# A hybrid decoder step on one core: both scans' stages of a turn in one row on TensorE, and pairs of PSUM banks begun together in the preparation

## The chip, the cores and the metric

The kernel runs on 1 core of one Trainium2 chip. The metric is the device time of one launch in microseconds (us). PE is TensorE, PEld its weight loads, DVE VectorE, ACT ScalarE, POOL GpSimd, SP SyncE; ACTq is ACT's sequencer when it issues a DMA.

## The reference

One layer of a decoder is computed for 1024 prompt tokens and 64 sample tokens (8 sequences of 8), all in fp32. The part that the change touches is the mixer: two recurrent scans that share one projection of the input and one projection of the output.

```python
proj = x @ w_in
o_a, ... = _rwkv7_mix(proj[..., :A_SHIFT_W], ...)          # mixer A: 8 heads of 64
o_b, ... = _gated_delta_mix(proj[..., A_SHIFT_W:], ...)    # mixer B: 4 heads of 128
mix = jnp.concatenate([o_a, o_b], axis=-1) @ w_o
x = _layer_norm(DN_ALPHA * x + mix, ln1_g, ln1_b)
ffn, f_conv_new = _conv_ffn(x, f_conv, w_up, f_conv_w, f_conv_b, w_down)
x = _layer_norm(DN_ALPHA * x + ffn, ln2_g, ln2_b)
e = _rms_norm(p @ w_ple, ple_g)
x = x + jax.nn.sigmoid(x @ w_ple_gate) * e
```

Mixer A updates a matrix state `S = S * w_t + sa (kk_t * a_t) + v_t k_t` token by token; mixer B works in chunks, `v_new = u_c - w_c @ S`, `o = q_c @ S + a_c @ v_new`, `S = S * gl + k_c^T v_new`, after a triangular solve in each chunk.

## The kernel before, in words

**Two kinds of work on PE.** The dense products (projections, output projection, feed-forward, gate) are fp32r products of 128x512: each weight and each activation is split into a high and a low part, and three products are added up. They are recorded on PE as `acc<-x,whi`, `acc<-x,wlo`, `acc<-whi,X` and so on, one record each. Everything of the two scans and their preparation is plain fp32, and each such product leaves two records on PE, a transpose one.

**Units.** The prompt is cut into two blocks of 512 tokens (`tb`), each into two halves of 256 (`half`), and the heads into two groups (`g`). `run` (L1609) goes through eight prompt units: for each block first both halves of group 0, then both of group 1, and then two small sample units. I number the prompt units 1 to 8; units 1 to 4 belong to the first block.

- `prep` (L1047) prepares a unit: shifts, gates and norms, then `a_gram` (L673: Gram products `aux<-AR,BK`, transposes `aux<-cst,BK` and `aux<-cst,tmp`), `b_gram` (L822: Gram products `aux<-BK,KN`, DVE's product into `MB`, transposes `aux<-cst,KN` and `aux<-cst,tmp`), and `invert` (L947). `invert` sends the triangular systems through DRAM (DMAs `inv_t`, then `iN`), solves 16x16 blocks on DVE in some 30 small steps from `iY<-iN` to `iN<-iY`, and loads the result back (DMAs `inv_x`, `inv_y`, then 8 loads `Dt<-inv_y` and 8 `Dd<-inv_x`), all DMAs issued by ACT.
- `merge` (L996) builds the inverses of the larger blocks from that: four rounds of PE products with an addition on DVE behind each (`aux<-Dt,MG`, `aux<-Dd,DX`, `aux<-Y,DX` twice), then three smaller steps. A row of a round begins with `touch` (L204, `aux<-zeros`), a product that waits for all that the row needs.
- `scan` (L1069) runs mixer A's four chunks and mixer B's two, with the merge of the next unit beside them.
- `out` (L899) normalises the outputs and writes them to DRAM; its first product on PE is `aux<-OA,cst`.

**The scans' stages.** `a_step` (L735) has three stages with a yield behind each: R (`scan<-S,AR`, `scan<-UV,MG`), solve (`scan<-RA,DX`), and out with the state (`scan<-AR,S`, `scan<-MG,UV` into one bank, `scan<-UV,BT` into another). `b_step` (L874) has R (`scan<-S,KN`), solve (`scan<-RB,DX`) and out with the state (`scan<-QE,S`, `scan<-MB,UB` into one bank, `scan<-UB,KD` into another), each followed by two yields. `together` (L717) advances all generators by one yield in each turn. So in turn 1 A's R meets B's R, in turn 3 A's out meets B's solve, in turn 5 A's solve meets B's out, and so twice per unit.

**PSUM.** There are eight banks: four of the pool `acc` for the dense products, two of `aux` for the preparation, the merge and `out`, two of `scan` for the scans. ACT or DVE must empty a bank before it is used again.

**What sets the order.** The kernel is written as a program whose instructions a list scheduler orders, engine by engine, by priority and by when operands are ready in its own model; each engine then runs its list strictly in order. Inside `fill` (L263) instructions get a low priority, so that dense products fill PE between the scans' steps. In the first block the fill is the rest of the projection of the second block and the embedding product; the output projection `dense_first` (L1410) can begin with the two features of 128 rows that group 0 wrote, and its further features, and all that comes behind it, need what the `out` of unit 4 writes. A row (`inrow`, L198) chains the matmuls issued in it, so that they keep the order in which they are written:

```python
def mm(s, out, lhsT, rhs, start=True, stop=True):
    i = s.nc.tensor.matmul(out, lhsT=lhsT, rhs=rhs, start=start, stop=stop)
    if s.row is not None:
        if s.row:
            s.tc.add_manual_dep(i.ins, s.row[-1], s.nosync, reason="order")
        s.row.append(i.ins.name)
```

A chain only says what comes first on PE. It does not forbid other instructions in between.

Of the kernel before, what the change touches and what calls it, by code (L numbers as in the profile page):

```python
# [145 lines left out]
class Kern:  # L146
# [40 lines left out]
        return s.bank("scan")  # L187

    def mm(s, out, lhsT, rhs, start=True, stop=True):
        i = s.nc.tensor.matmul(out, lhsT=lhsT, rhs=rhs, start=start, stop=stop)  # L190
        if s.row is not None:
            if s.row:
                s.tc.add_manual_dep(i.ins, s.row[-1], s.nosync, reason="order")
            s.row.append(i.ins.name)
        return i
# [15 lines left out]

    def tr(s, out, in_):
        k = in_.shape[0]
        s.nc.tensor.transpose(out, in_, s.ident[:k, :k])  # L214

    def act(s, out, in_, f=AF.Copy, **kw):
        s.nc.scalar.activation(out, in_, f, **kw)  # L217
# [455 lines left out]
    def a_gram(s, st, cm):  # L673
        nc = s.nc
        nch, AR, BK, Xv = st["nch"], st["AR"], st["BK"], st["Xv"]
        last = nc.cur_bb.bb.instructions[-1]
        MG = s.tl([128, NCH, 2, 2, 2, 64], "MG", 2)
        st["room"] = MG.rearrange("p c a s e t -> p (c a s e t)")[:, 512:1664].rearrange("p (i x) -> p i x", i=2)
        MG = MG[:, :nch]
        BT = s.tl([128, NCH, 2, 128], "BT", 2)[:, :nch]  # L680
        UV = s.tl([128, NCH, 2, 2, 64], "UV", 2)[:, :nch]
        for e in range(2):
            nc.gpsimd.memset(UV[64 * (1 - e):64 * (1 - e) + 64, :, :, e, :], 0.0)
        cc = min(nch, 2)
        n = 2 * cc
        mask = s.cst[:, cm:cm + 128].rearrange("p (s t) -> p s t", s=2).unsqueeze(1).broadcast_to([128, n, 2, 64])
        for c0 in range(0, nch, 2):
            bs = [s.bank() for _ in range(2)]
            with s.inrow():
                s.touch(bs[1], last)  # L690
                for i in range(n):
                    c, p = c0 + i // 2, i % 2
                    for e, b in enumerate(bs):
                        r = 64 * e
                        s.mm(b[:, i * 128:(i + 1) * 128], BK[r:r + 64, p, c, :, :], AR[r:r + 64, p, c, 1:3, :])
            for e, b in enumerate(bs):
                s.mul(MG.rearrange("p c a s e t -> p (c a) s e t")[:, 2 * c0:2 * c0 + n, :, e, :],
                      b[:, :n * 128].rearrange("p (h s t) -> p h s t", h=n, s=2), mask)
        for c0 in range(0, nch, 2):
            b = s.bank()  # L700
            for i in range(n):
                c, p = c0 + i // 2, i % 2
                s.tr(b[:, i * 128:(i + 1) * 128], BK[:, p, c, :, :].rearrange("p s t -> p (s t)"))
            s.act(BT[:, c0:c0 + cc].rearrange("p c a t -> p (c a t)"), b[:, :n * 128])

        b = s.bank()
        nq = nch // cc
        for i in range(2 * nq):
            q, p = i // 2, i % 2
            s.tr(b[:64 * cc, i * 128:(i + 1) * 128], Xv[:, p, q * 64 * cc:(q + 1) * 64 * cc])  # L710
        b = b[:, :nq * 256].rearrange("p (q a e v) -> p q a e v", q=nq, a=2, e=2)
        for e in range(2):
            for i in range(cc):
                s.act(UV[64 * e:64 * e + 64, i::cc, :, e, :], b[64 * i:64 * i + 64, :, :, e, :])
        st.update(MG=MG, BT=BT, UV=UV)

    def together(s, *gens):  # L717

        gens = list(gens)
        while gens:  # L720
            gens = [g for g in gens if next(g, True) is None]

    def a_solve(s, st, c, R):

# [97 lines left out]
    def b_gram(s, st, cn):  # L822
        nc = s.nc
        KN, KQ, Xv, tm, gd, t0, m, nq, g = (st[k] for k in ("KN", "KQ", "Xv", "tm", "gd", "t0", "L", "nq", "g"))
        q0 = t0 // 128
        n = 2 * nq
        hs = slice(2 * g, 2 * g + 2)
        M = s.tl([128, 2, 2, 2, LB], "MB", 2)[:, :nq, :, :, :m]
        KD = s.tl([128, 2, 256], "KD", 2)[:, :nq]
        VB = s.tl([128, 2, 256], "VB", 2)[:, :nq]  # L830
        E = s.tmp(128, nq, 2, m)
        for q in range(nq):
            nc.sync.dma_start(E[:m, q], gd[2:3, hs, t0 + q * m:t0 + (q + 1) * m].broadcast_to([m, 2, m]))
        for q in range(nq):
            for h in range(2):
                s.stt(E[:m, q, h, :], E[:m, q, h, :], tm[:m, q0 + q, 0, 2 * g + h:2 * g + h + 1], s.cst[:m, cn:cn + m],
                      ALU.subtract, ALU.add)
        Ef = E[:m].rearrange("p q h t -> p (q h) t")
        s.act(Ef, Ef, AF.Exp)
        for q in range(nq):  # L840
            b = s.bank()
            for h in range(2):
                s.mm(b[:m, h * 2 * m:(h + 1) * 2 * m], KN[:, h, q * m:(q + 1) * m], KQ[:, h, q, :, :])
            s.mul(M[:m, q], b[:m, :4 * m].rearrange("p (h s t) -> p h s t", h=2, s=2),
                  E[:m, q].unsqueeze(2).broadcast_to([m, 2, 2, m]))
        for src, dst, kind in ((KN, KD, 3), (Xv, VB, 1)):
            b = s.bank()
            for q in range(nq):
                for h in range(2):
                    j = 2 * q + h  # L850
                    s.tr(b[:m, j * 128:(j + 1) * 128], src[:, h, q * m:(q + 1) * m])
            s.mul(dst[:m].rearrange("p q (h d) -> p q h d", h=2), b[:m, :n * 128].rearrange("p (q h d) -> p q h d", q=nq, h=2),
                  tm[:m, q0:q0 + nq, kind, hs].unsqueeze(3).broadcast_to([m, nq, 2, 128]))
        st.update(MB=M, KD=KD, VB=VB)
# [214 lines left out]
    def scan(s, tb, half, g, st, ahead):  # L1069

        sa, sb, Z = st
        OA = s.tl([128, 2, MB], "OA")
        OB = s.tl([128, 2, MB], "OB")

        def a_all():
            for c in range(NCH):
                yield from s.a_step(sa, c, OA)
                yield

        def b_all():  # L1080
            for q in range(MB // LB):
                yield from s.b_step(sb, q, OB)

        s.together(a_all(), b_all(), *ahead)
        return OA, OB

    def mix_out(s, tb, half, g, st, o):
# [646 lines left out]
```

## Time and profile before

| | |
|---|---|
| median of 3 runs | 1921.58 us (1918.12 to 1926.15) |
| the profiled execution's own time | 1920.4 us |
| its span | 1918.6 us, 29879 instructions |
| PE busy | 1831.8 us (95%), 10446 records |
| DVE, ACT, POOL busy | 1269.8, 918.0, 154.7 us |
| granted clock of PE, mean | 0.989 |
| DMA | 255.88 MB, mean 133 GB/s |

A row of the timeline has the start of the first record, the time to the end of the last, engine, line, operation, what it writes and reads, shapes and the number of records; in brackets stands the engine's idle time before it and what ended that. Records of PE overlap: a product of 128x512 lasts about 0.4 us as a record, while the next begins 0.23 us later.

### The profile page before, as it was taken

The page shows a single profiled execution, that of the slowest core. Times are in us where ns is not written, and L with a number is a line of the kernel's source. Part 1 is how long each engine was busy: PE and PEld are TensorE (multiplying, and loading weights), DVE is VectorE, ACT ScalarE, POOL GpSimd, SP SyncE. Part 2 cuts the span into 40 slices and gives each one's busy share as a digit, 9 for nine tenths or more (in the row PEclk, how much of TensorE's full clock was granted, in tenths as well). Part 3 has the DMA queues.
Part 4 walks back from the last instruction along what each step waited for, and adds up shares of the span by engine and source line. Part 5 has one row for each costly group of instructions (what it writes and reads, how often), then busy time and mean ns, then how long its engine had stood idle before and what let it go on. Part 6 is the DMA issues. An engine that isn't in the chain of part 4 may idle for free. (4 is left out here: it accounts for less than half of the span.)

```text
span 1918.6 us, 29879 instructions
## 1 busy us (share of the span) xinstructions
PE 1831.8 (95%) x10446; PEld 1463.3 (76%) x10446; DVE 1269.8 (66%) x2748; ACT 918.0 (48%) x1814; POOL 154.7 (8%) x305
## 2 busy tenths in 40 slices
PE   9999999999799798999999999999999999999998
PEld 7878777777567577777887767777787888888877
DVE  4366566758586685877768767666857752455488
ACT  5454447465564744646455435543633332333372
POOL 2000010001000000000000000200212210111000
PEclk9999999999899899999999999999999999999999
DMA  6435342434444365442423446875332222222355
GB/s 216 152 123 153 112 113 89 137 100 133 144 138 145 126 181 163 129 114 82 117 81 112 131 137 194 274 246 200 134 119 92 96 78 83 83 78 79 114 174 165
DMA packets 219126, 255.88 MB, mean 133 GB/s; under 512 B 81848, under 2 KB 117096, under 8 KB 218976
## 3 DMA queue, kind: packets, MB, share of 16 engines
q1 hardware_dynamic: 162040, 246.36, 39.8%
q10 hardware_dynamic: 56936, 7.62, 2.5%
q8 instruction: 82, 1.34, 0.3%
q14 instruction: 68, 0.56, 0.1%
HBM read 200.64 MB, written 53.26 MB: 132 GB/s over the span
## 5 line engine op out<-in xcount | busy, mean ns | idle before, releaser
L190 PE MATMUL acc<-x,whi 128*128 128x512 f32 x2400 | 784.5, 403 | 7.9 <-ACT whi L217 5.1
L220 DVE TENSOR_TENSOR wlo<-wraw,whi 128x512 fp32r<-128x512 f32 (+1 forms) x462 | 323.2, 700 | 343.7 <-ACT whi L217 319.0
L217 ACT ACTIVATE whi<-wraw 128x512 fp32r<-128x512 f32 (+1 forms) x462 | 287.4, 623 | 497.8 <-PE acc L190 169.0
L190 PEld LDWEIGHTS acc<-x,whi 128*128 128x128 f32 x2400 | 429.5, 189 | 89.0 <-issue 7.8
L190 PE MATMUL acc<-x,wlo 128*128 128x512 f32 x1200 | 483.0, 403 | 0.0
L190 PEld LDWEIGHTS acc<-x,wlo 128*128 128x128 f32 x1200 | 226.9, 189 | 54.3 <-issue 6.0
L190 PE MATMUL acc<-whi,X 128*128 128x512 f32 x436 | 145.5, 407 | 9.5 <-ACT st L217 6.2
L217 ACT ACTIVATE st<-acc 128x512 f32<-128x512 f32 (+2 forms) x134 | 77.4, 595 | 62.3 <-PE acc L190 39.2
L190 PEld LDWEIGHTS acc<-whi,X 128*128 128x128 f32 x436 | 81.9, 191 | 29.8 <-ACT st L217 7.2
L190 PE MATMUL acc<-wlo,X 128*128 128x512 f32 x220 | 87.5, 398 | 0.0
L229 DVE SCALAR_TENSOR_TENSOR st<-st,par,st 128x512 f32<-128x512 f32 (+1 forms) x132 | 78.1, 593 | 2.8
L217 ACT ACTIVATE st<-st 128x512 f32<-128x512 f32 x66 | 33.3, 505 | 72.9 <-DVE st L229 68.4
L190 PE MATMUL scan<-whi,X 128*128 128x256 f32 (+2 forms) x208 | 62.4, 335 | 0.0
L217 ACT ACTIVATE tmp<-tmp 128x512 f32<-128x512 f32 (+4 forms) x75 | 40.5, 548 | 30.6 <-DVE tmp L229 22.7
L229 DVE SCALAR_TENSOR_TENSOR st<-st,st 128x512 f32<-128x512 f32 x74 | 40.6, 550 | 19.5 <-ACT st L217 18.6
L190 PE MATMUL scan<-whi,xsm 128*128 128x256 f32 x176 | 49.3, 281 | 2.4 <-ACT st L217 2.4
L190 PE MATMUL scan<-wlo,X 128*128 128x256 f32 (+2 forms) x164 | 51.5, 314 | 0.0
L217 ACT ACTIVATE X<-wraw 128x512 fp32r<-128x512 f32 (+1 forms) x65 | 40.5, 623 | 21.1 <-DMA wraw<-hd 10.7
L506 POOL COPY tail<-st 128x3 f32<-128x3 f32 x52 | 14.6, 283 | 436.6 <-ACT st L217 436.6
L220 DVE TENSOR_TENSOR X<-wraw,X 128x512 fp32r<-128x512 f32 x60 | 43.5, 724 | 9.4 <-ACT X L217 9.3
L217 ACT ACTIVATE tmp<-tmp,par 128x256 f32<-128x256 f32 (+1 forms) x100 | 43.0, 470 | 14.0 <-issue 4.5
L190 PE MATMUL scan<-wlo,xsm 128*128 128x256 f32 x176 | 49.5, 282 | 0.0
(358 smaller groups left out, 3306.9 us busy)
## 6 DMA issues: line engine op xcount, KB each, us to landing
wraw<-w_up SPq DMA_DIRECT2D x176, 256.0 KB
wraw<-w_in SPq DMA_DIRECT2D x112, 256.0 KB
wraw<-w_down SPq DMA_DIRECT2D x98, 256.0 KB
wraw<-hd SPq DMA_DIRECT2D x44, 256.0 KB
wraw<-w_o SPq DMA_DIRECT2D x32, 256.0 KB
wraw<-w_gate SPq DMA_DIRECT2D x32, 256.0 KB
hd<-st SPq DMA_DIRECT2D x22, 256.0 KB
st<-lnv SPq DMA_DIRECT2D x20, 256.0 KB
```

Source lines behind the costliest of these rows:

```text
L190: i = s.nc.tensor.matmul(out, lhsT=lhsT, rhs=rhs, start=start, stop=stop)
L217: s.nc.scalar.activation(out, in_, f, **kw)
L220: (eng or s.nc.vector).tensor_tensor(out, a, b, op)
L229: s.nc.vector.scalar_tensor_tensor(out, a, sc, b, op0, op1)
L506: s.nc.gpsimd.tensor_copy(s.tails[tb][:, f0 + f, :], st[:, TB - 3:TB])
```

## The change

`together` gets a parameter `join`: for the first `join` generators, here A's and B's scan, all matmuls that are issued in one turn are chained, B's first behind A's last. `mm` and `tr` both go through a new function `chain`, so that transposes can stand in a row too. In `a_gram` the two banks of transposes of BK, in `b_gram` the two banks of Gram products and the two banks of transposes are allocated first, filled in one row, and emptied afterwards. The arithmetic is the same, and so are the numbers of products.

```diff
+        return s.chain(s.nc.tensor.matmul(out, lhsT=lhsT, rhs=rhs, start=start, stop=stop))
+
+    def chain(s, i):
         if s.row is not None:
             if s.row:
                 s.tc.add_manual_dep(i.ins, s.row[-1], s.nosync, reason="order")
...
-        s.nc.tensor.transpose(out, in_, s.ident[:k, :k])
+        s.chain(s.nc.tensor.transpose(out, in_, s.ident[:k, :k]))
...
-        for c0 in range(0, nch, 2):
-            b = s.bank()
-            for i in range(n):
-                c, p = c0 + i // 2, i % 2
-                s.tr(b[:, i * 128:(i + 1) * 128], BK[:, p, c, :, :].rearrange("p s t -> p (s t)"))
+        bs = [s.bank() for _ in range(0, nch, 2)]
+        with s.inrow():
+            for c0, b in zip(range(0, nch, 2), bs):
+                for i in range(n):
+                    c, p = c0 + i // 2, i % 2
+                    s.tr(b[:, i * 128:(i + 1) * 128], BK[:, p, c, :, :].rearrange("p s t -> p (s t)"))
+        for c0, b in zip(range(0, nch, 2), bs):
             s.act(BT[:, c0:c0 + cc].rearrange("p c a t -> p (c a t)"), b[:, :n * 128])
...
-    def together(s, *gens):
+    def together(s, *gens, join=0):
         gens = list(gens)
+        head = gens[:join]
         while gens:
-            gens = [g for g in gens if next(g, True) is None]
+            left = []
+            last = None
+            for g in gens:
+                if g not in head:
+                    done = next(g, True)
+                elif last is None:
+                    s.row = []
+                    done = next(g, True)
+                    last = s.row[-1] if s.row else None
+                    s.row = None
+                else:
+                    s.row = [last]
+                    done = next(g, True)
+                    s.row = None
+                if done is None:
+                    left.append(g)
+            gens = left
...
-        for q in range(nq):
-            b = s.bank()
-            for h in range(2):
-                s.mm(b[:m, h * 2 * m:(h + 1) * 2 * m], KN[:, h, q * m:(q + 1) * m], KQ[:, h, q, :, :])
+        bs = [s.bank() for _ in range(nq)]
+        with s.inrow():
+            for q, b in enumerate(bs):
+                for h in range(2):
+                    s.mm(b[:m, h * 2 * m:(h + 1) * 2 * m], KN[:, h, q * m:(q + 1) * m], KQ[:, h, q, :, :])
+        for q, b in enumerate(bs):
...
+        todo = [(s.bank(), *v) for v in ((KN, KD, 3), (Xv, VB, 1))]
+        with s.inrow():
+            for b, src, dst, kind in todo:
...
-        s.together(a_all(), b_all(), *ahead)
+        s.together(a_all(), b_all(), *ahead, join=2)
```

**First place: PE in turn 5 of unit 4's scan,** A's solve and B's out. `RA` is A's right-hand side, `DX` the inverse, `QE` and `S` B's query and state, `MB` B's decayed Gram matrix, `UB` its solution, `KD` its keys; `acc` rows are dense products. Before:

```order
L190 MATMUL acc_3675<-whi_3678,X_3607 128x512
L190 MATMUL scan_6022<-RA_5988,DX_36_122 128x64 x2
L190 MATMUL scan_6028<-QE_4920,S_40_133 128x128
L190 MATMUL scan_6028<-MB_5087,UB_5952 128x128
L190 MATMUL scan_6028<-QE_4920,S_40_133 128x128
L190 MATMUL scan_6028<-MB_5087,UB_5952 128x128
L190 MATMUL scan_6027<-UB_5952,KD_5088 128x128 x2
L190 MATMUL acc_3675<-whi_3678,X_3607 128x512
```

The same stages with the change:

```order
L190 MATMUL acc_3878<-x_2666,whi_3898 128x512
L190 MATMUL scan_6022<-RA_5988,DX_36_122 128x64 x2
L190 MATMUL scan_6028<-QE_4920,S_40_133 128x128
L190 MATMUL scan_6028<-MB_5087,UB_5952 128x128
L190 MATMUL acc_3878<-x_2666,whi_3898 128x512
L190 MATMUL acc_3878<-x_2666,wlo_3899 128x512
L190 MATMUL scan_6027<-UB_5952,KD_5088 128x128
L190 MATMUL scan_6028<-QE_4920,S_40_133 128x128
L190 MATMUL scan_6028<-MB_5087,UB_5952 128x128
L190 MATMUL scan_6027<-UB_5952,KD_5088 128x128
L190 MATMUL acc_3877<-x_2666,whi_3898 128x512
```

The second head's products of the bank 6028 now stand behind the first product of the bank 6027, and two dense products stand between the two heads: what was one stretch of scan products is now two.

**Second place: PE at the merge of unit 5,** which runs beside unit 4's scan. `Dt` and `Dd` are what `invert` loads back, `zeros` the touch that waits for it; the `acc` rows with `X_6354` and `X_6377` are the output projection's first two features. Before:

```order
L190 MATMUL acc_6344<-wlo_6372,X_6377 128x512
L190 MATMUL aux_5871<-zeros_104 128x8
L190 MATMUL aux_5871<-Dt_120,MG_5685 64x64 x16
L190 MATMUL aux_5872<-Dt_120,MB_5762 64x64 x8
L190 MATMUL acc_6345<-whi_6348,X_6354 128x512 x2
L190 MATMUL acc_6345<-wlo_6349,X_6354 128x512
L190 MATMUL acc_6346<-whi_6348,X_6354 128x512 x2
L190 MATMUL acc_6346<-wlo_6349,X_6354 128x512
L190 MATMUL aux_5907<-zeros_104 128x8
L190 MATMUL aux_5907<-Dd_119,DX_35_121 64x64 x16
L190 MATMUL aux_5908<-Dd_119,DX_35_121 64x64 x8
```

With the change:

```order
L190 MATMUL acc_6346<-wlo_6372,X_6377 128x512
L190 MATMUL aux_5871<-zeros_104 128x8
L190 MATMUL aux_5871<-Dt_120,MG_5685 64x64 x16
L190 MATMUL aux_5872<-Dt_120,MB_5762 64x64 x8
L190 MATMUL aux_5907<-zeros_104 128x8
L190 MATMUL aux_5907<-Dd_119,DX_35_121 64x64 x16
L190 MATMUL aux_5908<-Dd_119,DX_35_121 64x64 x8
L190 MATMUL aux_5954<-zeros_104 128x8
L190 MATMUL aux_5954<-Y_5869,DX_35_121 64x64 x16
```

All dense products that unit 4's `out` does not hold back (the last is the second feature's, `X_6377`, in the bank 6346) now stand ahead of the merge, and none between its rounds.

## Rows read from the trace of the kernel before

**Rows 1.** The page's part 1: busy time, share, instructions.
```profile
PE 1831.8 (95%) x10446; PEld 1463.3 (76%) x10446; DVE 1269.8 (66%) x2748; ACT 918.0 (48%) x1814; POOL 154.7 (8%) x305
```
**Rows 2.** Windows, PE: window, its length, PE busy (records), granted clock, DMA share, GB/s.
```profile
404.66:507.10 102.44, 90.70 (x644) 0.97 0.42 126
507.10:628.81 121.71, 108.53 (x720) 0.97 0.42 133
628.81:760.63 131.82, 114.58 (x723) 0.92 0.54 167
760.63:873.00 112.37, 107.85 (x728) 1.00 0.40 116
```
**Rows 3.** Timeline of PE, 914 to 919 us: dense products and fp32 transposes.
```profile
914.72 0.60 PE L214 MATMUL aux<-cst,BK 128*128 128x128 f32 x4
915.16 0.39 PE L190 MATMUL scan<-UV,BT 128*128 128x128 f32 x2
915.38 0.60 PE L214 MATMUL aux<-cst,BK 128*128 128x128 f32 x4
...
916.41 0.71 PE L190 MATMUL acc<-x,whi 128*128 128x512 f32 x2
916.96 0.60 PE L214 MATMUL aux<-cst,tmp 128*128 128x128 f32 x4
917.31 0.47 PE L190 MATMUL acc<-x,wlo 128*128 128x512 f32 x1
917.62 0.62 PE L190 MATMUL acc<-x,whi 128*128 128x512 f32 x2
918.09 0.39 PE L190 MATMUL acc<-x,wlo 128*128 128x512 f32 x1
918.31 0.63 PE L190 MATMUL acc<-x,whi 128*128 128x512 f32 x2
```
**Rows 4.** Timeline of PE: unit 5's Gram products, its merge, unit 4's out.
```profile
574.06 1.97 PE L190 MATMUL aux<-BK,KN 128*128 128x256 f32 x8 [1.04 <-DVE BK L220]
...
612.29 0.17 PE L190 MATMUL aux<-zeros 128*128 128x8 f32 x1
...
628.81 1.08 PE L190 MATMUL aux<-OA,cst 128*128 128x512 f32 x2
```
**Rows 5.** Timeline of PE: unit 4's second Gram pair, its merge, unit 3's out.
```profile
450.74 1.13 PE L190 MATMUL aux<-BK,KN 128*128 128x256 f32 x4
...
489.56 0.34 PE L190 MATMUL aux<-zeros 128*128 128x8 f32 x1 [8.37 <-DMA Dt<-inv_y]
...
507.10 1.08 PE L190 MATMUL aux<-OA,cst 128*128 128x512 f32 x2
```
**Rows 6.** Timeline of DVE and ACT's queue: unit 5's inversion.
```profile
577.57 1.29 DVE L220 TENSOR_TENSOR MB<-aux,tmp 128x512 f32<-128x512 f32 x2
...
589.02 0.28 DVE L964 COPY iY<-iN 96x256 f32<-96x256 f32 x1
...
596.62 0.68 DVE L220 TENSOR_TENSOR wlo<-wraw,whi 128x512 fp32r<-128x512 f32 x1
...
601.76 0.38 DVE L977 COPY iN<-iY 96x256 f32<-96x256 f32 x1
...
606.37 1.30 ACTq L992 DMA_DIRECT2D Dt<-inv_y  x3
...
609.77 0.35 ACTq L992 DMA_DIRECT2D Dt<-inv_y  x1
```
**Rows 7.** Timeline of PE: unit 1's Gram products (two pairs) and its merge.
```profile
149.13 1.99 PE L190 MATMUL aux<-BK,KN 128*128 128x256 f32 x8 [0.22 <-ACT BK L217]
...
182.14 0.17 PE L190 MATMUL aux<-zeros 128*128 128x8 f32 x1
```
**Rows 8.** Timeline of PE: the wait for a bank of `acc`, 521.6 us.
```profile
521.58 1.22 PE L190 MATMUL acc<-whi,X 128*128 128x512 f32 x2 [5.16 <-ACT st L217]
```
**Rows 9.** Windows, PE: the stretches behind the waits of rows 5 and 8.
```profile
489.80:495.00 5.20, 5.20 (x81) 0.67 0.51 147
521.60:527.00 5.40, 5.40 (x18) 0.50 0.67 246
```
**Rows 10.** Timeline of PE: two waits inside the scans for ACT's copy of UV.
```profile
550.02 0.49 PE L190 MATMUL scan<-MG,UV 128*128 128x128 f32 x2 [1.73 <-ACT UV L217]
...
624.68 0.49 PE L190 MATMUL scan<-MG,UV 128*128 128x128 f32 x2 [0.37 <-ACT UV L217]
```

More of the change, by code (lines that the diff above doesn't have):

```diff
@@ L189, in mm @@
     def mm(s, out, lhsT, rhs, start=True, stop=True):
-        i = s.nc.tensor.matmul(out, lhsT=lhsT, rhs=rhs, start=start, stop=stop)
+        return s.chain(s.nc.tensor.matmul(out, lhsT=lhsT, rhs=rhs, start=start, stop=stop))
+    def chain(s, i):
         if s.row is not None:
@@ L839, in b_gram @@
         s.act(Ef, Ef, AF.Exp)
-        for q in range(nq):
-            b = s.bank()
-            for h in range(2):
-                s.mm(b[:m, h * 2 * m:(h + 1) * 2 * m], KN[:, h, q * m:(q + 1) * m], KQ[:, h, q, :, :])
+        bs = [s.bank() for _ in range(nq)]
[4 more added lines that the diff above has]
+        for q, b in enumerate(bs):
             s.mul(M[:m, q], b[:m, :4 * m].rearrange("p (h s t) -> p h s t", h=2, s=2),
                   E[:m, q].unsqueeze(2).broadcast_to([m, 2, 2, m]))
[L846 to L851, printed above, removed]
+        todo = [(s.bank(), *v) for v in ((KN, KD, 3), (Xv, VB, 1))]
+        with s.inrow():
+            for b, src, dst, kind in todo:
+                for q in range(nq):
+                    for h in range(2):
+                        j = 2 * q + h
+                        s.tr(b[:m, j * 128:(j + 1) * 128], src[:, h, q * m:(q + 1) * m])
+        for b, src, dst, kind in todo:
             s.mul(dst[:m].rearrange("p q (h d) -> p q h d", h=2), b[:m, :n * 128].rearrange("p (q h d) -> p q h d", q=nq, h=2),
```

## The prediction

> **What bounds the kernel now.** I read the page's engine part first, then windows of PE, then PE's timeline where its order changes, and DVE's and ACT's queue beside it. PE is busy for 1831.8 of 1918.6 us, 95% [rows 1], so the other engines matter only where PE waits for them. The windows say where that is: from unit 3's `out` to unit 4's PE is idle for 121.71 - 108.53 = 13.2 us, in the window ahead for 11.7, in the one behind for 17.2, but from unit 5's to unit 6's `out` only for 4.5 [rows 2]. Up to unit 4's `out` the dense products that may run are limited: the output projection can begin with two features and must wait with the others for that `out`. PE's time to that point is therefore the longer of two: its work, or the chain of unit 4's and unit 5's steps. The link of the chain that ends last is the inversion. From unit 4's second Gram pair to its merge 38.8 us pass, and PE stands still for 8.37 of them [rows 5]; for unit 5 the same way, 575.0 (the second half of the row of 1.97 us) to 612.3, takes 37.3 us and ends without a wait, because enough dense products stand between [rows 4].
>
> **What the change does, by the order.** Counts are from the two orders of PE's instructions, prices from the trace. I call a stretch of scan and preparation products between two dense ones a visit.
>
> *Visits.* The order before has 336, the new one 351: 15 more. A chain does not keep others out, so where a stage must wait for a bank, the scheduler still puts dense products in between, and now splits stages that could be reordered before. A's solve with B's out was one visit in 6 of 16 turns and is one in none (the first place shows one); A's out with B's solve falls from 3 to 1; only the two R stages gain, from 12 to 14. The price of a visit: between 916.41 and 917.62 us three dense products and four transposes run in 1.21 us; three dense products take 0.69 by themselves (917.62 to 918.31), four transposes inside a visit 0.44 (914.72 to 915.16) [rows 3]. That leaves 0.07 us. 15 visits cost 1.1 us; the ends are 0 and 15 x 0.37 = 5.5, if each begins with the smaller wait of [rows 10].
>
> *Turn 5.* B's first `UB,KD` now stands ahead of the second head. In all 16 turns dense products stand between it and the first head's product, in 10 of them only one or two (0.23 to 0.47 us); the bank may still hold A's solve until ACT has copied it. The nearest rows are the two waits for that copy, 0.37 and 1.73 us [rows 10]. The ends are 0 and 10 x 1.73 = 17 us. I take 1.3, three or four of the smaller wait, since before such places were mostly passed without one.
>
> *The preparation's pairs.* Transposes and Gram products are the same in number. The two transposed banks of a unit were contiguous in 5 of 9 cases and still are, the Gram pairs go from 5 to 6. Nothing is taken for them: their visits are already in the 15, and ACT and DVE empty the banks one behind the other as before.
>
> *Where the dense products stand.* This is the largest term. Ahead of unit 3's `out` the new order has 1295 dense products of 512 columns against 1260, 35 more; from there to unit 5's second Gram pair 155 against 112, 43 more; from there to unit 5's merge 70 against 136; between the rounds of that merge and unit 4's `out` none against 12 (the second place). The sum is the same, so nothing is won by running them earlier, and the chain of steps begins later on PE. Step by step, with 0.23 us for a dense product and 0.22 for an fp32 one [rows 3]:
> - Unit 4's merge has ten dense products less above it and four fp32 products more, 1.4 us less cover, and PE waits there already [rows 5]: 1.4 us more. Unit 3's `out` comes at 507.1 + 35 x 0.233 + 1.4 = 516.7 us.
> - To unit 5's second Gram pair it took 575.0 - 507.1 = 67.9 us [rows 4, 5]. The 43 products add 10.0 us and four scan products 0.9. On the way lie waits that the extra products may cover: 5.16 us for a bank of `acc` [rows 8], the 2.7 us that half a clock cost behind it (5.4 us at 0.50 [rows 9]), 1.73 us for ACT [rows 10] and 1.04 for the operand [rows 4], 10.6 in all. I take half, 5.3: 516.7 + 67.9 + 10.9 - 5.3 = 590.2 us.
> - The inversion needs at most 37.3 us there. Its DVE part, 589.0 to 601.8 us [rows 6], holds four splits of weights and one of activations of 0.68 us; the new order has one, since the dense products have run out. So 37.3 - 4 x 0.7 = 34.4 us, and the merge can begin at 624.6. PE has 18.4 us of work until then and stands still for some 16. The ends of the latency are 32.0 us (unit 1's, from 150.1 to 182.1, where PE came without waiting [rows 7]) and 38.8 [rows 5].
> - From the merge to unit 4's `out` it took 16.5 us [rows 4], with 12 dense products (2.8 us) between the rounds. Without them the additions on DVE lie bare: between 13.7 and 16.5, I take 15.1. Behind the waits of 8.37 and 5.16 us the granted clock was 0.67 for 5.2 us and 0.50 for 5.4 [rows 9], losses of 1.7 and 2.7 us of the 2.4 GHz level; I add 1.7. Unit 4's `out`: 624.6 + 15.1 + 1.7 = 641.4 us against 628.81, **12.6 us later**.
> - From there PE has the same work left in both orders, so this isn't given back.
>
> The ends of this term: all 10.6 us covered, no more wait at unit 4's merge, 32.0 us and 13.7 give 629.2 (0.4 later); none covered, 38.8, 16.5 and 2.7 give 653.5 (24.7 later).
>
> *Units 6 to 8.* By the same count the cover of the merge grows or stays for units 6 and 7, and falls by 2.5 us for unit 8, where PE waited for less than 1 us: 0 to 2.5 more, I take 1.2.
>
> **Sum.** 12.6 + 1.2 + 1.1 + 1.3 = 16.2 us. The profiled execution's own time is 1920.4 us (its span is 1918.6), so 1936.6 us. It stands 1.2 us below the median of the runs shown, 1921.6, which changes nothing at this precision.
>
> **The rivals.**
>
> *Starved elsewhere as much as before: no change, about 1922 us.* If the extra products cover all four waits ahead of unit 5's Gram products and the inversion is as short as unit 1's, the term is 0.4 us and only the visits are left, 1.5 us. For it speaks that PE did wait for operands there, 1.04 us [rows 4], so that a later place on PE is partly free; against it that the inversion took over 37 us in two of the three places read.
>
> *Faster, about 1908 us.* The window behind unit 4's `out` loses the most, 17.2 us idle and 8% of the clock over 114.6 busy us, 9 us [rows 2]; the next one does the same kind of work with 4.5 idle at full clock. If the changed order of ACT and DVE makes it as smooth, 12.7 + 9 = 22 us are won there. It decides once the starved stretch costs less than half of its 12.6 us: with 6 us there and 3.6 for the other terms, 1920.4 + 9.6 - 22 = 1908. Against it: PE's order right behind that `out` is almost the same in both (29 dense products for 27 ahead of the first break), so most of these waits have no reason to go.
>
> *Banks as the bound, slower still, about 1955 us.* A joined turn has three groups of products for two banks of `scan`, so it can only be one visit by waiting for ACT in the middle. If the waits of [rows 10] stand in all 32 joined turns of turns 3 and 5 at the mean of the two, 1.05 us, they cost 34 us, and the sum becomes 1920.4 + 34 with hardly anything of the starved stretch. The Trainium skill's page "Perfetto Trace Analysis", section "Matmuls", says the same of any kernel: independent groups should rotate through different PSUM banks, so that one's evacuation runs beside the next one's products. By that rule alone joining these stages would cost that much, 1955 us; by the trace and the order it costs 1.3, because in all 16 cases of turn 5 and 15 of 16 of turn 3 dense products stand in the gap.
>
> *The change doesn't do what it says* is not a rival but part of my forecast: by the order the stages are not one visit.
>
> **How the numbers follow.** The starved stretch at about its size: 0.60, of which 0.07 stays below +0.5%. Nothing changes: 0.19. Faster: 0.12. Banks: 0.09. Half a per cent, 9.6 us, is about what a measurement of this kernel can tell from no change; so slower 0.53 + 0.09 = 0.62, same 0.26, faster 0.12. The likeliest case's own range is 1922 to 1950 us: its ends, with the visits' and unit 8's. For 8 in 10 I go down to 1912, which leaves out most of the faster case, and keep 1950, which leaves out the bank case.
>
> **What would show it.** Right: PE waits over 10 us for `Dt<-inv_y` at unit 5's merge, at a clock near 0.5 to 0.7 behind it; the windows' ends show unit 3's `out` near 517 and unit 4's near 641 us; the later windows are within 4 us of before. Wrong: no such wait, or unit 4's `out` before 633 us; waits by ACT of a microsecond in most of the scans' turns (the bank rival); or the window behind unit 4's `out` shorter by over 10 us (the faster one).

## The result and the profile after

The changed kernel takes 1935.43 us (median of 7 runs, 1929.73 to 1939.92) against 1924.32 (7 runs) of the kernel before: a ratio of 1.0064, 95% interval 1.0041 to 1.0086, about 12 us slower. The profiled execution took 1936.16 us, its span is 1934.4.

Windows of PE in the kernel after, in the columns of [rows 2]: from the start to unit 3's and to unit 4's `out`, then from each unit's `out` to the next one's, from unit 1's on:

```profile
0.00:529.75 529.75, 495.84 (x3222) 0.98 0.44 133
...
0.00:645.85 645.85, 594.23 (x3903) 0.98 0.43 130
...
303.20:420.09 116.89, 110.24 (x740) 0.99 0.39 110
...
420.09:529.75 109.66, 94.68 (x644) 0.94 0.44 134
529.75:645.85 116.10, 98.39 (x684) 0.96 0.39 117
645.85:773.37 127.52, 113.20 (x713) 0.91 0.56 168
773.37:891.86 118.49, 108.49 (x720) 0.96 0.36 108
```

The three of the kernel before that [rows 2] lack:

```profile
0.00:507.10 507.10, 481.08 (x3186) 0.99 0.43 134
...
300.77:404.66 103.89, 102.49 (x715) 1.00 0.39 121
0.00:628.81 628.81, 589.60 (x3904) 0.99 0.43 134
```

Unit 4's `out` comes at 645.85 us instead of 628.81, 17.0 later, and the span is 15.8 longer: the loss is made ahead of that `out`, and the 1288.6 us behind it are 1.2 shorter than before. Up to there both kernels have run the same products (3903 and 3904 records). So the 17.0 us split into idle time, 645.85 - 594.23 = 51.6 against 39.2, 12.4 more, and into the same products taking longer, 594.23 - 589.60 = 4.6.

Unit 3's `out` tells where most of it is lost. It comes at 529.75 us instead of 507.10, 22.65 later. Of that, 8.1 us are the 35 dense products that now run ahead of it and no longer behind it. The other 14.5 us are lost: 7.9 of idle time (33.9 against 26.0) and 6.6 by products that took longer. About half of the 14.5 is lost between unit 1's and unit 2's `out` already, a window 13.0 us longer with 25 records more (an estimate of 5.8 us at 0.23 each). From unit 3's `out` to unit 4's, the stretch in which the moved products are missing, only 2.5 us are lost.

What PE waited for up to unit 4's `out`, after (engine, bank, line, what it waited for: us in total, times, longest):

```profile
PE aux L190 <- DMA Dd<-inv_x: 16.2, 3, 11.8
...
PE acc L190 <- ACT st L219: 3.5, 2, 2.6
PE scan L190 <- DVE st L222: 2.9, 2, 1.8
PE scan L190 <- ACT OA L219: 2.7, 2, 1.6
PE scan L190 <- ACT OB L219: 2.7, 1, 2.7
PE scan L190 <- DVE S L222: 1.9, 2, 1.2
PE scan L190 <- ACT UV L219: 1.7, 2, 1.4
PE scan L190 <- DVE S L231: 1.6, 2, 1.4
```

The same view before:

```profile
PE aux L190 <- DMA Dt<-inv_y: 8.4, 1, 8.4
PE acc L190 <- ACT st L217: 6.2, 3, 5.2
...
PE scan L190 <- ACT UV L217: 2.3, 3, 1.7
PE scan L190 <- DVE RA L746: 2.0, 1, 2.0
...
PE scan L190 <- DVE iY L220: 1.0, 1, 1.0
```

Added up over all lines of the two views, waits at the merges grow from 8.4 to 16.2 us and waits of scan products from 8.5 to 16.1; waits for banks of `acc` fall from 11.6 to 8.0. At unit 5's merge the wait grows from none to 11.8 us, and this is the wait that was forecast; at unit 4's it falls from 8.4 to 4.2, where the forecast had 1.4 more. PE's timeline has the first, and the windows show the clock around it:

```profile
599.06 1.13 PE L190 MATMUL aux<-BK,KN 128*128 128x256 f32 x4
629.54 0.35 PE L190 MATMUL aux<-zeros 128*128 128x8 f32 x1 [11.78 <-DMA Dd<-inv_x]
```
```profile
620.00:625.00 5.00, 0.00 (x0) 0.81 0.16 42
625.00:630.00 5.00, 0.46 (x5) 0.50 0.27 25
630.00:635.00 5.00, 4.31 (x97) 0.67 0.13 12
```

The scans' share was not forecast at this size. Its longest piece, on PE and then on ACT:

```profile
481.02 0.38 PE L190 MATMUL scan<-UB,KD 128*128 128x128 f32 x2
481.24 0.39 PE L190 MATMUL scan<-QE,S 128*128 128x128 f32 x2
481.47 0.39 PE L190 MATMUL scan<-MB,UB 128*128 128x128 f32 x2
481.69 0.39 PE L190 MATMUL scan<-UB,KD 128*128 128x128 f32 x2
484.80 0.49 PE L190 MATMUL scan<-AR,S 128*128 128x128 f32 x2 [2.72 <-ACT OB L219]
```
```profile
483.33 0.63 ACT L219 ACTIVATE whi<-wraw 128x512 fp32r<-128x512 f32 x1 [3.39 <-DMA wraw<-w_ple]
483.87 0.61 ACT L219 ACTIVATE tmp<-tmp 4x512 f32<-4x512 f32 x1
484.39 0.36 ACT L219 ACTIVATE OB<-scan 128x256 f32<-128x256 f32 x1
```

B's out runs head by head, as it is now chained. A's out of the next turn stands right behind it, without a dense product between, and needs the bank that B's out has just filled. ACT would empty it (`OB<-scan`), but stands 3.39 us at a weight that has not landed, with that copy queued behind. The Trainium skill's page "Perfetto Trace Analysis", section "Matmuls", asks that one group's evacuation run beside another group's products; at this place no product runs beside it, and PE stands still for 2.72 us.

### The profile page after: what moved, and what is told of

The parts are those of the page before. It is cut to its first block, busy times and chain, and to the rows that moved or that the text cites. A ratio compares the mean times of both kernels' runs of the same rounds, so it can differ in the third digit from the quotient of the medians.

```text
span 1934.4 us, 29896 instructions
## 1 busy us (share of the span) xinstructions
PE 1840.0 (95%) x10446; PEld 1470.4 (76%) x10446; DVE 1268.9 (66%) x2748; ACT 923.5 (48%) x1817; POOL 159.0 (8%) x305
## 5 line engine op out<-in xcount | busy, mean ns | idle before, releaser
L508 POOL COPY tail<-st 128x3 f32<-128x3 f32 x52 | 16.2, 318 | 481.4 <-ACT st L219 481.4
L190 PEld LDWEIGHTS acc<-wlo,X 128*128 128x128 f32 x220 | 42.6, 194 | 9.1 <-DVE wlo L222 0.2
L190 PE MATMUL scan<-wlo,xsm 128*128 128x256 f32 x176 | 49.3, 281 | 0.0
L190 PE MATMUL aux<-tmp,cst 128*128 128x512 f32 (+1 forms) x80 | 39.1, 589 | 9.2 <-DVE tmp L231 5.1
```

The source lines that it names most:

```text
L190: return s.chain(s.nc.tensor.matmul(out, lhsT=lhsT, rhs=rhs, start=start, stop=stop))
L508: s.nc.gpsimd.tensor_copy(s.tails[tb][:, f0 + f, :], st[:, TB - 3:TB])
```

## The experiments

Each ratio is to the kernel before on the same chip. *Counted work* in the expectations is the number of products in PE's order times the prices of [rows 3]. Theory 1 was that the dense products, moved ahead of unit 3's `out`, are missing at unit 5's merge; theory 2 that a chained stage waits in its middle, wherever it stands. The diffs are against the change unless the text says otherwise.

**The pairs alone.**

```diff
-        s.together(a_all(), b_all(), *ahead, join=2)
+        s.together(a_all(), b_all(), *ahead)
```

> The preparation's pairs alone (transposes and Gram products of two banks in one row each), the scans' turns as before. By the orders every engine's sequence is the same as before, PE's, DVE's, ACT's, GpSimd's and SyncE's. Every theory: the time of before, a ratio within 0.2% of 1; anything beyond that would be the measurement's own uncertainty.

Measured: 1923.48 us, 1.0000 (0.9986 to 1.0014). This part is worth nothing. It also tells how far a single trace can be trusted: with the same order, unit 4's `out` came at 628.37 (before 628.81), but the span was 1924.3 (1918.6).

**One of the two scans chained, not joined.** `head[0]` is A, `head[1]` B:

```diff
-                elif last is None:
+                elif g is head[0]:
                     s.row = []
                     done = next(g, True)
-                    last = s.row[-1] if s.row else None
                     s.row = None
                 else:
-                    s.row = [last]
                     done = next(g, True)
-                    s.row = None
```

> Pairs as in the change; in a turn only the first head group's (A's) stages are chained, B's are free and nothing is joined. By the order 336 visits, as before the change, and 31.7 us of counted PE work between unit 5's second Gram pair and its merge, where before has 34.6 and the change 18.4. Theory 1 (the time went where the dense products were moved from, at unit 5's merge): within 4 us of before, 1920 to 1928, the wait at unit 5's merge under 7 us. Theory 2 (a chained stage itself waits in its middle for ACT or DVE, so that each chained turn costs): about half of the change's loss, 5 to 6 us, since half of the stages are chained.

> Pairs as in the change; only the second group's (B's) stages are chained, A's are free and nothing is joined. By the order 359 visits, unit 3's out has 8.4 us more counted work ahead of it than in before (the change: 8.1 in unit 2 and 8.1 in unit 3), and only 16.1 us of counted work stand between unit 5's second Gram pair and its merge. Theory 1: a wait of 14 us or more at that merge and a time at least that of the change, 1936 to 1942 us. Theory 2: about half of the change's loss, 1928 to 1930. Counting visits at the change's own 0.7 us each (11 us for 15): 23 more, 1940 us.

Measured: A alone 1922.85 us, 0.9999 (0.9985 to 1.0012); B alone 1942.22, 1.0113 (1.0088 to 1.0137), more than the change. So it is not the half of the stages that costs half: A's chain costs nothing, B's everything. The wait at unit 5's merge is 3.9 us with A alone, as theory 1 had it, and 11.8 with B alone, where theory 1 had 14 or more. With A alone all merge waits together grow to 14.2 us from 8.4 without a loss; with B alone they are 17.0 and the scan waits 13.3 (table below). The trace of B alone has 58 records more ahead of unit 3's `out` than before (3244 against 3186), 13.2 us of counted work where the expectation says 8.4. Counting visits gave 1940 us for it, which fits as well; the joined turns below decide that.

**Chained, but not joined.**

```diff
-                    s.row = [last]
+                    s.row = []
```

> The change, but A's and B's stages of a turn are each chained by themselves and not joined. By the order 349 visits, the same counted work ahead of every out as in the change, and 19.6 us between unit 5's second Gram pair and its merge. Theory 1: as the change within 3 us, 1932 to 1938, with a wait of 10 to 12 us at that merge; so joining, which the change is named after, costs nothing by itself. Rival (the joint between A and B is what waits): the loss is gone by half or more, under 1930.

Measured: 1936.67 us, 1.0080 (1.0063 to 1.0097), the wait at unit 5's merge 10.7 us. Joining A's and B's stages, after which the change is named, adds nothing to the chains; theory 1's time and wait came, and the joint is out.

**B's out and A's out written in another order.** In `a_step` the products into `b` get a loop of their own behind those into `bo`; in `b_step` likewise:

```diff
             s.mm(bo[:, hc], S[:, h, :], QE[:, h, ts], True, False)
             s.mm(bo[:, hc], U[:, hc], M[:, q, h, 1, :], False, True)
+        for h in range(2):
+            hc = slice(h * 128, (h + 1) * 128)
             s.mm(b[:, hc], KD[:, q, hc], U[:, hc])
```

> The change, with the products of the out stages written in another order: those of both heads into the output bank first, then those into the state bank. By the order 331 visits and 32.3 us between unit 5's second Gram pair and its merge (before 34.6), 4.1 us more counted work ahead of unit 3's out than before instead of 8.1, although the stages are chained and joined as in the change. Theory 1: the time of before, 1918 to 1926, the wait at unit 5's merge under 6 us. Theory 2 (chained stages wait in their middle): as the change, 1932 to 1938. Counting visits at 0.7 us: 5 fewer than before, 1920.

Measured: 1932.32 us, 1.0054 (1.0037 to 1.0072): 10 us over the kernel before, so theory 1 as put missed in the time, though the wait at unit 5's merge is 3.6 us, under its 6. The time just reaches the range of theory 2, but not by its mechanism: up to unit 4's `out` at 639.71 the merges wait 7.1 us and the scans 6.2, both less than before. What grew are waits for `acc` banks, 17.6 us against 11.6, and the products' own time, 597.0 us against 589.6, with a granted clock of 0.94 in both windows from unit 2's to unit 4's `out` (before 0.97, [rows 2]). PE's timeline has the waits; the first is new, the last stands where the kernel before waits 5.16 us [rows 8]:

```profile
493.99 1.22 PE L190 MATMUL acc<-whi,X 128*128 128x512 f32 x2 [5.22 <-ACT st L219]
502.29 0.35 PE L190 MATMUL aux<-zeros 128*128 128x8 f32 x1 [3.54 <-DMA Dt<-inv_y]
...
535.70 0.77 PE L190 MATMUL acc<-whi,X 128*128 128x512 f32 x1 [4.68 <-ACT st L219]
```

That the merge wait is *the* cause falls here; it is one form that the loss can take.

**Where the joined turns stand.**

```diff
-        s.together(a_all(), b_all(), *ahead, join=2)
+        s.together(a_all(), b_all(), *ahead, join=2 if 4 * tb + 2 * g + half < 3 else 0)
```

The condition is `> 2` for the second run and `== 0` for the third.

> The change, with the scans' turns joined in units 1 to 3 alone; from unit 4 on the turns are as before. By the order 336 visits, as before the change; the same counted work ahead of the outs of units 1 to 4 as in the change, 19.0 us between unit 5's second Gram pair and its merge (the change 18.4, before 34.6). If the loss is made ahead of unit 4's out (scan waits of some 7 us in units 2 and 3, and the wait at unit 5's merge): all of the change's loss or more, 1934 to 1940, unit 4's out 15 to 18 us later than before. If it is the number of visits (0.7 us each): none, 1921 to 1926.

> The change, with the scans' turns joined from unit 4 on alone; in units 1 to 3 as before. By the order 348 visits, 12 more than before; the counted work ahead of the outs of units 1 to 4 as before, 32.5 us between unit 5's second Gram pair and its merge (before 34.6). If the loss is made ahead of unit 4's out: the time of before within 4 us, 1919 to 1927, and the windows of units 6 to 8 together not longer than before. If it is the number of visits: 8 us slower, 1932. If every joined turn costs (five of the eight units are joined): 6 to 8 us, 1930 to 1932.

> The change, with the scans' turns joined in unit 1 alone. By the order 333 visits; 2.8, 8.4 and 6.0 us more counted work ahead of the outs of units 1, 2 and 3 than before (the change: 2.8, 8.4, 8.1), 29.9 us between unit 5's second Gram pair and its merge. If the scan waits of units 2 and 3 come from dense products that now stand earlier: they come here too, some 7 us. If they come from the joined turns of units 2 and 3 themselves: the scan waits stay at those of before (under 2 us more), the wait at unit 5's merge is under 4 us, and the time is 2 to 6 us above before, 1924 to 1929.

Measured: units 1 to 3 alone 1942.38 us, 1.0100 (1.0082 to 1.0117); from unit 4 on 1924.44, 1.0006 (0.9989 to 1.0023). PE's merge of unit 5 in the first:

```profile
627.74 0.35 PE L190 MATMUL aux<-zeros 128*128 128x8 f32 x1 [10.79 <-DMA Dd<-inv_x]
```

and in the second:

```profile
612.60 0.24 PE L190 MATMUL aux<-zeros 128*128 128x8 f32 x1 [2.65 <-DMA Dt<-inv_y]
```

This pair settles the place: the first has no more visits than the kernel before and the whole loss, the second has 12 more visits and five joined units and no loss. The place was expected of both; it rules out visits and theory 2 in its general form. Two details missed: the first is 2.4 us above its range, and the second's windows of units 6 to 8 are together 274.5 us against 270.3, where not longer was expected, while the window ahead of them is 7.6 us shorter. Unit 1 alone joined gave 1943.28 us, 1.0092, but with a wide interval (1.0055 to 1.0128): its six executions lie between 1926.63 and 1950.31. Here the expectation missed. The scan waits stay low as the second reading said (9.8 us), and the merge of unit 5 waits only 3.5; yet unit 4's `out` is 10.8 us late: many smaller waits grew, 2.2 us at the merges, 1.3 in the scans, 3.8 for `acc`, and the rest for `aux`. This trace is of an execution of 1930.75 us, the second fastest of the six, so what the slower ones lost is not seen.

**The limit on the dense products taken away.** In the kernel before and in the change:

```diff
-                            s.dense_first(KT, s.hload(s.od[0]), I["w_o"], I["xp"], s.x1p)
+                            s.dense_first(KT, s.hload(I["xT"][:, :, 0:TB]), I["w_o"], I["xp"], s.x1p)
```

> The kernel before, but the output projection of the first block reads its input from the tensor xT, which is there from the start, instead of the mixer's output: it no longer waits for unit 4's out. (Left out: the use of the mixer's output for that block.) 345 visits, unit 4's out has 3.7 us more counted work ahead of it. Theory 1 (waits and half clock ahead of unit 4's out are lost because the dense products that may run there are limited): the 8.37 us at unit 4's merge shrink below 3 and the time falls by 5 to 20 us, to 1902 to 1917. Counting visits at 0.7 us: 9 more than before, 1928.

> The change with the same edit as in the run of the kernel before with a free output projection (left out: the use of the mixer's output for the first block). By the order 342 visits, 30 us more counted work ahead of unit 4's out than in the change and 40.0 us between unit 5's second Gram pair and its merge (the change 18.4). Theory 1: no wait over 3 us at unit 5's merge, and the time within 5 us of the freed kernel before; the change's loss of 11 us is gone or nearly so. Theory 2 (chained stages wait in their middle): it stays 8 to 12 us above the freed kernel before, since every turn is still chained.

Measured: the kernel before so freed 1915.34 us, 0.9957 (0.9943 to 0.9972), so the limit does cost it time, though not at unit 4's merge, which still waits 8.24 us. The change so freed 1934.70, 1.0060 (1.0044 to 1.0076): 19 us over the freed kernel before, where theory 1 gave at most 5 and theory 2 8 to 12. The trace says why. At unit 5's merge PE waits 1.71 us and for another reason:

```profile
642.47 0.24 PE L190 MATMUL aux<-zeros 128*128 128x8 f32 x1 [1.71 <-DMA wraw<-xT]
```

and at unit 8's `out` the two freed kernels are level: 1054.12 against 1026.34 us, 27.8 later with 28.3 us more counted work done. But those dense products are then missing between the outs of the two sample units; the window of this run, and that of the freed kernel before:

```profile
1128.58:1174.41 45.83, 35.78 (x183) 0.70 0.48 147
```
```profile
1100.63:1144.73 44.10, 42.93 (x251) 1.00 0.45 136
```

With 68 records less (15.9 us at 0.233 each, an estimate) the window is 1.7 us longer: 17.6 us of the profiled pair's 21.6. The shortage has moved on, not gone. The scan waits up to unit 4's `out` stay (13.7 us against 7.6 in the freed kernel before), so they don't hang on the wait at unit 5's merge.

**The inverse's transfers issued by two engines.** In the kernel before and in the change:

```diff
-                        i = s.uq.dma_start(D[rows, :, cols], d[y:y + nh].rearrange("y r t -> r y t"))
+                        i = (nc.gpsimd if D is s.Dd else s.uq).dma_start(D[rows, :, cols], d[y:y + nh].rearrange("y r t -> r y t"))
```

> The kernel before with one edit: of the 16 transfers that bring a unit's inverse blocks back (eight to Dt, eight to Dd), all issued one behind the other by ACT at 0.47 us each (8 in 3.77 us in the trace of before), the eight to Dd are issued by GpSimd. By the order 326 visits, 28.7 us between unit 4's second Gram pair and its merge (before 28.0), 32.4 for unit 5 (34.6). If the end of the inversion sets the start of the merge: the 8.37 us wait at unit 4's merge falls to 4 to 5 us and the time by 3 to 8, to 1914 to 1919. If GpSimd issues each slower than ACT, or the transfers themselves are what lasts: no gain, 1920 to 1926.

> The change with the same edit: the eight transfers to Dd issued by GpSimd. By the order 346 visits and 17.4 us between unit 5's second Gram pair and its merge (the change 18.4). Theory 1 (PE stands at unit 5's merge until the inversion's last transfer is there): the wait of 11.8 us falls by about 3.5 and the time with it, 1929 to 1933. If the wait is not the inversion's chain but the loss lies in the scan's turns: 1934 to 1938 as the change.

Measured: 1945.10 us, 1.0112 (1.0099 to 1.0125), and 1941.03, 1.0090 (1.0075 to 1.0104): both slower than any range expected, and in the change the wait did not shrink:

```profile
622.99 0.34 PE L190 MATMUL aux<-zeros 128*128 128x8 f32 x1 [12.54 <-DMA Dt<-inv_y]
```

The expectation overlooked the code: the first round's `touch` waits for the eight transfers to `Dt` alone, and ACT had issued those ahead of seven of the eight to `Dd` already. So this wait is the inversion's latency and not the issuing of `Dd`: from unit 5's second Gram pair to the merge 30.4 us pass, in the change 30.5. In the kernel before the merge waits did fall, from 8.4 to 2.1 us, but the waits for `acc` rose from 11.6 to 20.5. Ahead of unit 4's `out` 11.2 of its 21 us are lost; the rest was not followed.

Up to unit 4's `out` all twelve kernels whose output projection is not freed run the same products. In the order of that `out` (us; waits from the view shown above; the counted work ahead of unit 3's `out` is given over that of the kernel before; the last column is how much later than before that `out` comes, less this work):

| kernel | unit 4's out | PE busy | idle | merge | scan | `acc` | work moved ahead of unit 3's out | lost ahead of unit 3's out |
|---|---|---|---|---|---|---|---|---|
| pairs alone | 628.4 | 589.5 | 38.9 | 8.7 | 7.4 | 11.8 | 0 | 0.4 |
| before | 628.8 | 589.6 | 39.2 | 8.4 | 8.5 | 11.6 | 0 | 0 |
| joined from unit 4 on | 629.2 | 590.7 | 38.5 | 11.0 | 8.7 | 11.2 | 0 | 2.1 |
| A chained | 630.3 | 590.7 | 39.6 | 14.2 | 7.5 | 10.8 | 0.2 | 2.4 |
| joined in unit 1 | 639.6 | 591.0 | 48.6 | 10.6 | 9.8 | 15.4 | 6.0 | 7.6 |
| reordered outs | 639.7 | 597.0 | 42.8 | 7.1 | 6.2 | 17.6 | 4.8 | 9.0 |
| before, two issuers | 640.0 | 595.9 | 44.1 | 2.1 | 9.9 | 20.5 | 3.0 | 11.0 |
| the change, two issuers | 640.7 | 595.2 | 45.5 | 13.8 | 7.6 | 10.8 | 10.9 | 6.5 |
| chained, not joined | 643.6 | 592.5 | 51.1 | 15.1 | 14.6 | 9.8 | 8.1 | 13.0 |
| the change | 645.9 | 594.2 | 51.6 | 16.2 | 16.1 | 8.0 | 8.1 | 14.5 |
| joined in units 1 to 3 | 645.9 | 596.6 | 49.3 | 15.1 | 13.2 | 8.0 | 8.1 | 12.1 |
| B chained | 650.3 | 594.9 | 55.4 | 17.0 | 13.3 | 9.8 | 13.2 | 12.8 |

No kernel that leaves the dense products in their place is late, and every one that moves 3 us or more ahead of unit 3's `out` is late by 11 to 22 us. How late does not follow the amount: 3.0 us moved go with 11.2 us, 10.9 with 11.9. In each of these eight kernels the greater part is lost ahead of unit 3's `out`, so ahead of the stretch in which the moved products are missing. In which kind of wait it shows differs.

## Why the prediction was right, and where it was not

The forecast of 1936.6 us fell 1.2 us over the median, in its likeliest case. That it fell so near is in part luck, twice over. The forecast loss was 16.2 us, and the profiled pair has 15.8; but the medians are 11.1 apart (about 12 by the ratio), and the nearness comes from a base of 1920.4 us, 3.9 below the median of the kernel before in that comparison. And most of the loss lies at another place than forecast: of its 12.6 us up to unit 4's `out`, the forecast put 1.4 ahead of unit 3's and 11.2 behind it, where the trace has 14.5 and 2.5. The starved merge is there, with its wait and the low clock behind it, and the forecast had the direction from it; but it is not where most of the time goes. Step by step:

- *The pairs at nothing:* right, a ratio of 1.0000.
- *Visits, 1.1 us:* small, as taken (the three times give 1.21 - 0.69 - 0.44 = 0.08 us a visit and not 0.07, which adds 0.1). Twelve more of them with the joined turns from unit 4 on measure 1.9 us, interval -2.1 to 4.4, and units 1 to 3 give the whole loss with none.
- *Unit 4's `out` 12.6 us later:* 17.0, but by two errors that partly cancel. The step "Unit 3's `out` comes at 507.1 + 35 x 0.233 + 1.4 = 516.7 us" failed: it came at 529.75, 13.1 later. Behind it all went faster than forecast: 69.3 us to unit 5's second Gram pair (forecast 73.5), since 9.5 of the 10.6 us were covered of which half had been counted on, the 5.16 for `acc` [rows 8] entirely; 30.5 to the start of its merge, below the 32.0 that was kept as the lower end (forecast 34.4; 37.3 - 4 x 0.7 is 34.5); 16.3 from there to the `out` (16.8). PE stood still for 11.8 us at that merge instead of 16.
- *Turn 5, 1.3 us:* mis-sized, and part of the reason for the 13.1. Up to unit 3's `out` the waits of scan products grew by 7.0 us (12.8 against 5.8) and those for `acc` by 3.1, while the merge waits fell by 4.0; the products that took 6.6 us longer make the other half. Among the scans' waits are those of A's out behind B's out, 2.72 us at 484.80 and 1.44 at 440.91. All waits of scan products up to unit 4's `out` grew by 7.6 us, inside the ends that were kept (0 to 17). "Banks as the bound" was held against the forecast as a rival of 34 us; it was in fact a part of it, at less than a quarter of that size.
- *The clock, 1.7 us:* too little. The same products took 4.6 us longer up to unit 4's `out`, 6.6 longer ahead of unit 3's and 2.0 shorter behind it; the forecast had a loss behind the long wait alone. The window from unit 2's to unit 3's `out` has 0.94 where [rows 2] have 0.97. In it lies a stretch with four waits of 0.9 to 4.2 us at a mean clock of 0.83, between the levels of 1.2 and 2.4 GHz; the kernel before has 0.90 in its own such stretch. As an estimate that is 6.8 us of full clock against 3.3:

```profile
480.00:520.00 40.00, 29.39 (x200) 0.83 0.58 182
```
```profile
474.00:507.00 33.00, 24.21 (x282) 0.90 0.55 167
```

- *Units 6 to 8, 1.2 us:* the time behind unit 4's `out` is 1.2 us shorter in the profiled pair, less than the 5.7 by which two profiles of one order differed. The check that each later window stays within 4 us failed for the one from unit 5's `out`, 118.49 against 112.37 us [rows 2], while the one ahead is 4.3 shorter, far from the 22 us of the rival that was faster. Both belong to the joined turns of the later units: with those alone they are 118.5 and 124.2 us.
- *The change doesn't do what it says:* right, and the run without the joint shows that it would not matter.

What is shown: the loss is made ahead of unit 4's `out`, by the turns of units 1 to 3; the chain on B's stages is enough for it, A's costs nothing, and joining the two adds nothing. What is not shown: that dense products moved early are its common cause. That rests on the table and on the pair of early and late turns; no run moves these products alone, and the scheduler orders ACT's and DVE's queues anew with them. Why 14.5 us are lost ahead of unit 3's `out`, and why the same shift ends now as a wait at the merge, now for `acc`, and now as longer products, stays open.

## What to carry to other kernels

Fillers that run out before the chain they cover are a budget: an edit that only reorders the small steps can spend them early, and a wait then turns up where they are missing. Here that wait came as forecast, but more time was lost in the stretches ahead of it. So measure the loss at a point up to which both kernels have run the same products, then stretch by stretch, with the moved work taken off, before naming the step that costs it. A chain is such an edit: it takes freedom from the scheduler even where it keeps no other product out.

## What the runs showed of the hardware

In some kernels the executions differ mostly in the granted clock, in others not. In the 17 executions of the kernel before beside the runs on the place of the joined turns, the span went from 1914.9 us (mean granted clock 0.990) to 1927.9 (0.983), while span times clock stayed between 1889 and 1898, all but one from 1894 on. With unit 1 alone joined the spans were 1924.8 (0.991) to 1948.5 (0.979), 24 us apart with the same instructions, and the product 1904 to 1908. In the changed kernel, however, the product ranges from 1898 to 1907, nearly as far as the spans, 1927.9 to 1938.1. A wait behind which the clock is low costs more than its idle time: around and behind the one at unit 5's merge the windows above have 0.50 and 0.67.

ACT's queue couples things that share no data: a scan's bank was late by 2.72 us because ACT stood for 3.39 us at a weight that the scan does not need.
